# Differential attention with later transposes and one shared PSUM bank per head, and another order of the three branch projections

## The chip, the cores and the metric

The kernel runs on one core of one Trainium2 chip. The metric is the time of one execution on the device in microseconds (us). A core has five engines that run side by side, each through its own instructions in a fixed order: TensorE (PE, matmuls and transposes; its weight loads are the row PEld), VectorE (DVE), ScalarE (ACT), GpSimd (POOL) and SyncE (SP, here the queue that issues most loads). TensorE writes to PSUM, which has eight banks of 128 x 512 float32.

## The reference

One decoder layer on 512 tokens of width 1024. One projection `x @ w_in` gives the inputs of three token mixers and three gates. Their results are projected, gated and summed, and one more projection, a LayerNorm, an MLP with a gated embedding and a second LayerNorm follow. What the change touches is the first mixer, differential attention with 4 heads, and the sum of branches:

```python
prob = softmax(logits + bias)                       # two maps per head, causal
w = prob[:, :, 0] - lam * prob[:, :, 1]
o = einsum('bhqk,bhkd->bhqd', w, v)
o = o * rsqrt(mean(square(o), axis=-1) + RMS_EPS) * norm_g * (1.0 - lam_init)
...
merged = (g[:, :, 0] * (o_da @ w_branch_da) + g[:, :, 1] * (o_sb @ w_branch_sb)
          + g[:, :, 2] * (o_dl @ w_branch_dil))
```

The mean in the norm goes over the 128 columns of one token of one head.

## The kernel before, in words

The big products run as a list of **items**, in order: 128 x 512 results, each made by 24 matmuls for the input projection (three for each of 8 slices of the depth: high part times high part and the two cross terms, lines 86 to 89 and 299 to 301), or by 12 for a branch projection. Each item has `mm`, which issues its matmuls into one of two PSUM banks (tag `mm`), and `ev`, which evacuates the bank when the next item begins. Weights come through SP as 512 KB loads into a ring, and are split into a high and a low part by ACT (line 209) and DVE (line 210) some items ahead.

**Attention** is written as Python generators: `sb_head` (stick-breaking, 8), `dil_head` (dilated, 4) and `da_block` (differential attention, 4 heads of 4 query blocks of 128 tokens). A call of `step()` (line 1137) advances each active generator to its next `yield`, and admits one more from `waiting` if the estimates of PSUM banks in use (2 for a `da_block`) sum to no more than 8. `step()` is called once ahead of an item's matmuls and once in their middle (lines 1179 to 1183), so a `yield` puts about 12 matmuls between two parts of a block. All attention parts take their PSUM from a pool of six banks (tag `at`). A scheduling layer then fixes the order of each engine's instructions, and gives a PSUM bank or a slot of SBUF to each tile when its last user is done.

One `da_block(hd, qb)` does this. It makes the logits of both maps (lines 138 and 139, into two banks), adds the bias and takes row maxima (DVE, line 945), takes exponentials with row sums (ACT, line 951), and combines the maps (DVE, lines 954 to 957). After one `yield`, TensorE transposes the 128 x 128 blocks of the weights (line 961), ACT or DVE copies them to SBUF (`wT`, line 963, through lines 96 and 98). After another `yield`, TensorE multiplies by the values (line 969, `po`, a bank of its own for each block), ACT takes the sum of squares (`scr`, line 976), DVE, POOL and DVE turn it into the norm and scale the block (lines 977, 978, 979). When all four blocks of a head are done, TensorE transposes them (line 985), and ACT and DVE write the high and low part (lines 987, 988), which the branch projection reads.

`branch_items(j)` (line 347) appends three items for each of eight column tiles `j`: differential attention (i = 0), stick-breaking (1), dilated (2). Each `ev` takes a sigmoid of the gate (line 344, ordered behind the last exponential of line 951), multiplies (line 361) and adds (line 365); the third splits the sum (lines 370, 371). Six gate items (two column tiles) stand ahead of the first branch item, the other gate items follow between the branch items. At the first branch item (line 1158) all generators that are left are run to their end before the item is issued.

Of the kernel before, what the change touches and what calls it, by code (L numbers as in the profile page):

```python
# [12 lines left out]
AF = mybir.ActivationFunctionType  # L13
OP = mybir.AluOpType
# [3 lines left out]
P = 128  # L18
FF = 4096
ALPHA = 2.0 ** 0.25  # L20
EPS = 1e-5
# [34 lines left out]
def trunk(tc, a, out):  # L56
    nc = tc.nc
    es = ExitStack()
    with es:
# [23 lines left out]
        def at_bank():  # L83
            return psum.tile([P, 512], F32, name=nm("at"), tag="at", bufs=6)
# [80 lines left out]
        def chunk(src, w):  # L165
            return chunk_of(load(src, w))
# [58 lines left out]
        def item(cs, mm, ev, need=None, bank=None):  # L225
            items.append({"c": cs, "mm": mm, "ev": ev, "need": need, "bank": bank})
# [12 lines left out]
        V = {}  # L239
# [94 lines left out]
        oTs = {}  # L334
# [12 lines left out]
        def branch_items(j):  # L347
            c1 = chunk(a["wb1"][j].rearrange("p k m -> p (k m)"), 1024)
            c2 = chunk(a["wb2"][j].rearrange("p k m -> p (k m)"), 512)
            for i in range(3):  # L350
                def mm(ps, i=i):
                    c = c2 if i == 2 else c1
                    for k in range(4):
                        s = slice(((i % 2) * 4 + k) * P, ((i % 2) * 4 + k) * P + P)
                        h, lo = oTs[4 * i + k]
                        mm3(ps, c["h"][:, s], c["l"][:, s], h, lo, k == 0, k == 3)

                def ev(ps, i=i):
                    gate_sig(i, j)
                    g = sg.pop((i, j))  # L360
                    nc.vector.tensor_mul(g, g, ps)
                    if i == 0:
                        merged[j] = g
                    else:
                        nc.vector.tensor_add(merged[j], merged[j], g)
                    if i == 2:
                        m = merged[j]
                        h = slot("mh", F32R)
                        lo = slot("ml", F32R)
                        nc.scalar.copy(h, m)  # L370
                        nc.vector.tensor_sub(lo, m, h.bitcast(F32))
                        merged[j] = (h, lo)
                item([c1, c2] if i == 2 else [], mm, ev, need=[c1, c2])

        first_branch = [None]
        LEAD = 2
# [361 lines left out]
        ident = one.tile([P, P], F32, name="ident")  # L738
# [3 lines left out]
        mhalf = one.tile([P, 1], F32, name="mhalf")  # L742
# [79 lines left out]
        for i in range(2):  # L822
            nc.vector.scalar_tensor_tensor(lamt[:, 2 * i, :], lamt[:, 2 * i, :], 1.0, lamt[:, 2 * i + 1, :],
                                           op0=OP.mult, op1=OP.mult, accum_out=lp[:, i:i + 1])
# [103 lines left out]
            yield  # L928


        da_on = {}
        da_left = {}

        def da_block(hd, qb):
            while ("da_q", hd) not in T or ("da_k", hd) not in T:
                yield
            n = (qb + 1) * P
            nk = max(n, 256)
            lg, ssum, mx = [], small("ss", 2), small("mx", 2)
            for m in range(2):  # L940
                ps = at_bank()
                mm_pair(ps[:, :nk], T["da_q", hd], T["da_k", hd], m, slice(qb * P, qb * P + P), slice(0, nk),
                        True, True)
                t = slot("lg")[:, :n]
                nc.vector.tensor_tensor_reduce(out=t, in0=ps[:, :n], in1=tab_da[hd][:, 384 - 128 * qb:512],
                                               scale=1.0, scalar=-3.0e38, op0=OP.add, op1=OP.max,
                                               accum_out=mx[:, m:m + 1])
# [9 lines left out]
            nc.vector.scalar_tensor_tensor(lg[0], lg[0], r[:, 0:1], lg[1], op0=OP.mult, op1=OP.add)  # L957
            yield
            tp = at_bank()
            for b in range(qb + 1):  # L960
                nc.tensor.transpose(tp[:, b * P:b * P + P], lg[0][:, b * P:b * P + P], ident)
            wT = slot("wT")[:, :n]
            cp(wT, tp[:, :n])
            yield
            while ("da_v", 0, qb) not in V:
                yield
            po = at_bank()
            for kb in range(qb + 1):
                nc.tensor.matmul(po[:, :P], wT[:, kb * P:kb * P + P], V["da_v", 0, kb][:, hd * P:hd * P + P],
                                 start=kb == 0, stop=kb == qb)  # L970
            if hd not in da_on:
                da_on[hd] = slot("on")
                da_left[hd] = 4
            scr = one.tile([P, P], F32, name=nm("scr"), tag="scr", bufs=2)
            ss = small("ms", 1)
            nc.scalar.activation(scr, po[:, :P], AF.Square, accum_out=ss)
            nc.vector.tensor_scalar(ss, ss, 1.0 / P, EPS, op0=OP.mult, op1=OP.add)
            nc.gpsimd.tensor_tensor(ss, ss, mhalf, OP.pow)
            nc.vector.tensor_scalar(da_on[hd][:, qb * P:qb * P + P], po[:, :P], ss, None, op0=OP.mult)
            da_left[hd] -= 1  # L980
            yield
            if da_left[hd] == 0:
                tp = at_bank()
                for b in range(4):
                    nc.tensor.transpose(tp[:, b * P:b * P + P], da_on[hd][:, b * P:b * P + P], ident)
                h, lo = slot("oTh", F32R), slot("oTl", F32R)
                nc.scalar.activation(h, tp, AF.Copy, scale=gcol)
                nc.vector.scalar_tensor_tensor(lo, tp, gcol, h.bitcast(F32), op0=OP.mult, op1=OP.subtract)
                oTs[hd] = (h, lo)
                yield  # L990


        def dil_head(hd):
# [143 lines left out]
        def step():  # L1137
            clock[0] += 1
            if waiting and sum(e[0] for e in active) + waiting[0][0] <= BANKS and clock[0] - last[0] >= GAP[0]:
                active.append(waiting.popleft() + (clock[0],))  # L1140
                last[0] = clock[0]
            for e in list(active):
                if (clock[0] - e[3]) % e[2]:
                    continue
                try:
                    next(e[1])
                except StopIteration:
                    active.remove(e)
# [7 lines left out]
        prev = None  # L1156
        for n, it in enumerate(items):
            if n == first_branch[0]:
                while active or waiting:
                    step()  # L1160
            need = it["need"] or it["c"]
            while any("h" not in c for c in need):
                pump(freed, 1)
            if prev is not None:
                prev[0]["ev"](prev[1])
            pump(freed)
            if n == 14:
# [119 lines left out]
```

## Time and profile before

| what | value |
|---|---|
| three runs, median (lowest to highest) | 1104.25 us (1103.94 to 1104.48) |
| the profiled execution's own time | 1104.82 us |
| its span, first to last instruction | 1103.1 us |
| mean granted TensorE clock | 0.996 of full |
| PE busy | 1084.1 us (98%) |
| DVE, ACT, POOL busy | 682.4, 481.7, 38.8 us |
| first and last transpose of line 961 | 379.9 and 484.1 us |

A view of the profile groups instructions, or gives the busy time of each engine in a stretch of the span. Behind a bar or in brackets stands the idle time just before an instruction, and the engine, tile and line that ended it. A matmul of 512 columns is recorded with 0.39 us, but the next one starts about 0.23 us after it, since they are pipelined.

### The profile page before, as it was taken

The page shows a single profiled execution, that of the slowest core. Times are in us where ns is not written, and L with a number is a line of the kernel's source. Part 1 is how long each engine was busy: PE and PEld are TensorE (multiplying, and loading weights), DVE is VectorE, ACT ScalarE, POOL GpSimd, SP SyncE. Part 2 cuts the span into 40 slices and gives each one's busy share as a digit, 9 for nine tenths or more (in the row PEclk, how much of TensorE's full clock was granted, in tenths as well). Part 3 has the DMA queues.
Part 4 walks back from the last instruction along what each step waited for, and adds up shares of the span by engine and source line. Part 5 has one row for each costly group of instructions (what it writes and reads, how often), then busy time and mean ns, then how long its engine had stood idle before and what let it go on. Part 6 is the DMA issues. An engine that isn't in the chain of part 4 may idle for free.

```text
span 1103.1 us, 13166 instructions
## 1 busy us (share of the span) xinstructions
PE 1084.1 (98%) x5032; PEld 898.6 (81%) x5032; DVE 682.4 (62%) x1216; ACT 481.7 (44%) x803; POOL 38.8 (4%) x74
## 2 busy tenths in 40 slices
PE   8999999999999999899999999999999999999996
PEld 5888788999888887778888888888888888888884
DVE  6868466564253758654444354875676686686676
ACT  7656444343232545453233232333554454454433
POOL 1000200000000000000000020110000000000000
PEclk9999999999999999999999999999999999999999
DMA  8222422131222103113322344243222322322302
GB/s 271 103 96 84 135 77 77 39 102 50 98 77 87 59 27 105 58 52 102 105 86 96 105 143 163 77 153 113 97 96 77 134 96 80 131 96 95 115 1 76
DMA packets 31327, 105.71 MB, mean 96 GB/s; under 512 B 3962, under 2 KB 4106, under 8 KB 31264
## 3 DMA queue, kind: packets, MB, share of 16 engines
q1 hardware_dynamic: 28080, 96.48, 25.6%
q0 software_dynamic: 2608, 7.35, 2.2%
q10 hardware_dynamic: 576, 1.05, 0.3%
q8 instruction: 39, 0.64, 0.2%
q14 instruction: 24, 0.20, 0.1%
HBM read 102.74 MB, written 2.12 MB: 95 GB/s over the span
## 4 chain that ended last, share of the span: by engine, by line
PE 90%; DVE 5%; ACT 2%; issue 1%; DMA 1%; POOL 1%; SPq 0%; DVEq 0%; ACTq 0%; POOLq 0%
PE mm L88 17%; PE mm L89 17%; PE mm L87 17%; PE mm L299 3%; PE mm L301 3%; PE mm L300 3%; PE mm L632 2%; PE mm L631 2%; PE mm L633 2%; PE at L632 2%; PE at L631 2%; PE at L633 2%; PE mm L462 1%; PE mm L460 1%; PE mm L527 1%; PE mm L528 1%
## 5 line engine op out<-in xcount | busy, mean ns | idle before, releaser
L209 ACT CAST wh<-raw 128x1024 fp32r<-128x1024 f32 (+2 forms) x176 | 180.4, 1027 | 295.9 <-PE mm L88 237.9
L210 DVE TENSOR_TENSOR wl<-raw,wh 128x1024 fp32r<-128x1024 f32 (+2 forms) x176 | 209.0, 1192 | 120.8 <-ACT wh L209 119.2
L87 PE MATMUL mm<-xhT,wh 128*128 128x512 f32 x512 | 203.1, 397 | 0.9 <-DVE da_qb L108 0.7
L88 PE MATMUL mm<-xlT,wh 128*128 128x512 f32 x512 | 200.9, 392 | 1.6 <-DVE xlT L210 1.6
L89 PE MATMUL mm<-xhT,wl 128*128 128x512 f32 x512 | 201.2, 393 | 0.5 <-DVE wl L210 0.5
L88 PEld LDWEIGHTS mm<-xlT,wh 128*128 128x128 f32 x512 | 96.5, 188 | 22.4 <-DVE xlT L210 3.5
L87 PEld LDWEIGHTS mm<-xhT,wh 128*128 128x128 f32 x512 | 96.6, 189 | 20.6 <-DVE da_qb L108 1.1
L89 PEld LDWEIGHTS mm<-xhT,wl 128*128 128x128 f32 x512 | 96.3, 188 | 20.5 <-DVE wl L210 1.0
L88 PE MATMUL mm<-x1lT,wh 128*128 128x512 f32 x256 | 99.6, 389 | 0.0
L89 PE MATMUL mm<-x1hT,wl 128*128 128x512 f32 x256 | 99.6, 389 | 0.0
L87 PE MATMUL mm<-x1hT,wh 128*128 128x512 f32 x256 | 99.6, 389 | 0.0
L299 PE MATMUL mm<-wh,xhT 128*128 128x512 f32 x160 | 65.5, 410 | 0.0
L300 PE MATMUL mm<-wl,xhT 128*128 128x512 f32 x160 | 63.2, 395 | 0.0
L301 PE MATMUL mm<-wh,xlT 128*128 128x512 f32 x160 | 63.2, 395 | 0.0
L87 PEld LDWEIGHTS mm<-x1hT,wh 128*128 128x128 f32 x256 | 48.1, 188 | 10.0
L89 PEld LDWEIGHTS mm<-x1hT,wl 128*128 128x128 f32 x256 | 48.1, 188 | 10.0
L88 PEld LDWEIGHTS mm<-x1lT,wh 128*128 128x128 f32 x256 | 48.1, 188 | 9.9
L209 ACT CAST wh<-wsum 128x1024 fp32r<-128x1024 f32 x28 | 29.5, 1053 | 52.7 <-PE mm L88 49.3
L210 DVE TENSOR_TENSOR wl<-wsum,wh 128x1024 fp32r<-128x1024 f32 x28 | 34.3, 1224 | 23.7 <-ACT wh L209 23.1
L638 DVE TENSOR_TENSOR xn<-xn,mm 128x512 f32<-128x512 f32 x56 | 38.2, 682 | 9.9 <-PE mm L633 9.8
L632 PE MATMUL mm<-wl,hh 128*128 128x512 f32 x112 | 43.6, 389 | 0.0
L631 PE MATMUL mm<-wh,hh 128*128 128x512 f32 x112 | 43.6, 389 | 0.0
(302 smaller groups left out, 1948.9 us busy)
## 6 DMA issues: line engine op xcount, KB each, us to landing
raw<-in_wt_dram SPq DMA_DIRECT2D x63, 512.0 KB, 3.3
raw<-in_wu_dram SPq DMA_DIRECT2D x32, 512.0 KB, 3.3
raw<-in_wd_dram SPq DMA_DIRECT2D x32, 512.0 KB, 3.2
raw<-in_wv_dram SPq DMA_DIRECT2D x20, 512.0 KB, 3.3
raw<-in_wb_dram SPq DMA_DIRECT2D x8, 512.0 KB, 3.3
raw<-in_wo_dram SPq DMA_DIRECT2D x8, 512.0 KB, 3.6
raw<-in_wg_dram SPq DMA_DIRECT2D x8, 512.0 KB, 5.0
rawx<-in_xT_dram SPq DMA_DIRECT2D x8, 256.0 KB, 7.2
```

Of the source, the lines that this page charges most:

```text
L87: nc.tensor.matmul(ps, wh, xh, start=start, stop=False, skip_group_check=True)
L88: nc.tensor.matmul(ps, wh, xl, start=False, stop=False, skip_group_check=True)
L89: nc.tensor.matmul(ps, wl, xh, start=False, stop=stop, skip_group_check=True)
L209: nc.scalar.copy(h, raw)
L210: nc.vector.tensor_sub(lo, raw, h.bitcast(F32))
L299: nc.tensor.matmul(ps, x1, c["h"][:, s], start=k == 0, stop=False)
L300: nc.tensor.matmul(ps, x1, c["l"][:, s], start=False, stop=False)
L301: nc.tensor.matmul(ps, x2, c["h"][:, s], start=False, stop=k == 7)
L631: nc.tensor.matmul(ps, h[:, q], c["h"][:, s], start=go, stop=False, skip_group_check=True)
L632: nc.tensor.matmul(ps, h[:, q], c["l"][:, s], start=False, stop=False, skip_group_check=True)
L633: nc.tensor.matmul(ps, lo[:, q], c["h"][:, s], start=False, stop=end, skip_group_check=True)
L638: nc.vector.tensor_add(t, t, ps)
```

## The change

1. In `da_block`, the one `yield` between the combined weights and their transposes becomes three.
2. The four blocks of a head write their values into four quarters of one PSUM bank (`da_po[hd]`), which the head keeps until its norm is done. The sums of squares go into four columns of one tile. The scale is computed once per head: one DVE operation on 128 x 4, one POOL power on 128 x 4, and one DVE multiplication of 128 x 512 with the four columns broadcast. Two more `yield`s stand ahead of the head's transposes.
3. The branch items come in the order stick-breaking, dilated, differential attention.
4. At the first branch item only the results of the other two mixers are waited for; the generators left are run to their end at the third.

```diff
-            for i in range(3):
+            for n, i in enumerate((1, 2, 0)):
...
-                    if i == 0:
+                    if n == 0:
                         merged[j] = g
...
-                item([c1, c2] if i == 2 else [], mm, ev, need=[c1, c2])
+                item([c1, c2] if n == 2 else [], mm, ev, need=[c1, c2])
...
             nc.vector.scalar_tensor_tensor(lg[0], lg[0], r[:, 0:1], lg[1], op0=OP.mult, op1=OP.add)
-            yield
+            for _ in range(3):
+                yield
             tp = at_bank()
...
-            po = at_bank()
+            if hd not in da_po:
+                da_po[hd] = at_bank()
+                da_left[hd] = 4
+                da_ss[hd] = small("ms", 4)
+            po = da_po[hd]
+            qs = slice(qb * P, qb * P + P)
             for kb in range(qb + 1):
-                nc.tensor.matmul(po[:, :P], wT[:, kb * P:kb * P + P], V["da_v", 0, kb][:, hd * P:hd * P + P],
-                                 start=kb == 0, stop=kb == qb)
+                nc.tensor.matmul(po[:, qs], wT[:, kb * P:kb * P + P], V["da_v", 0, kb][:, hd * P:hd * P + P],
+                                 start=kb == 0, stop=kb == qb, skip_group_check=True)
...
-            nc.scalar.activation(scr, po[:, :P], AF.Square, accum_out=ss)
-            nc.vector.tensor_scalar(ss, ss, 1.0 / P, EPS, op0=OP.mult, op1=OP.add)
-            nc.gpsimd.tensor_tensor(ss, ss, mhalf, OP.pow)
-            nc.vector.tensor_scalar(da_on[hd][:, qb * P:qb * P + P], po[:, :P], ss, None, op0=OP.mult)
+            nc.scalar.activation(scr, po[:, qs], AF.Square, accum_out=ss[:, qb:qb + 1])
             da_left[hd] -= 1
-            yield
             if da_left[hd] == 0:
+                yield
+                nc.vector.tensor_scalar(ss, ss, 1.0 / P, EPS, op0=OP.mult, op1=OP.add)
+                nc.gpsimd.tensor_tensor(ss, ss, mhalf.to_broadcast([P, 4]), OP.pow)
+                on = slot("on")
+                nc.vector.tensor_mul(on.rearrange("p (b d) -> p b d", b=4), po.rearrange("p (b d) -> p b d", b=4),
+                                     ss.unsqueeze(2).to_broadcast([P, 4, P]))
+                yield
+                yield
                 tp = at_bank()
...
             if n == first_branch[0]:
+                while any(4 + k not in oTs for k in range(8)):
+                    step()
+            if n == first_branch[0] + 2:
                 while active or waiting:
                     step()
```

More of the change, by code (lines that the diff above doesn't have):

```diff
@@ L356, in mm, with ev @@
                         mm3(ps, c["h"][:, s], c["l"][:, s], h, lo, k == 0, k == 3)
-                def ev(ps, i=i):
+                def ev(ps, i=i, n=n):
                     gate_sig(i, j)
@@ L365, in ev @@
                         nc.vector.tensor_add(merged[j], merged[j], g)
-                    if i == 2:
+                    if n == 2:
                         m = merged[j]
@@ L928, in sb_head @@
             yield
-        da_on = {}
+        da_po = {}
+        da_ss = {}
         da_left = {}
@@ L966, in da_block @@
                 yield
-            po = at_bank()
-            for kb in range(qb + 1):
-                nc.tensor.matmul(po[:, :P], wT[:, kb * P:kb * P + P], V["da_v", 0, kb][:, hd * P:hd * P + P],
-                                 start=kb == 0, stop=kb == qb)
-            if hd not in da_on:
-                da_on[hd] = slot("on")
-                da_left[hd] = 4
-            scr = one.tile([P, P], F32, name=nm("scr"), tag="scr", bufs=2)
[L975 to L979, printed above, removed]
+            if hd not in da_po:
[4 more added lines that the diff above has]
+            qs = slice(qb * P, qb * P + P)
+            for kb in range(qb + 1):
+                nc.tensor.matmul(po[:, qs], wT[:, kb * P:kb * P + P], V["da_v", 0, kb][:, hd * P:hd * P + P],
+                                 start=kb == 0, stop=kb == qb, skip_group_check=True)
+            scr = one.tile([P, P], F32, name=nm("scr"), tag="scr", bufs=2)
+            ss = da_ss[hd]
+            nc.scalar.activation(scr, po[:, qs], AF.Square, accum_out=ss[:, qb:qb + 1])
             da_left[hd] -= 1
-            yield
             if da_left[hd] == 0:
+                yield
[6 more added lines that the diff above has]
+                yield
                 tp = at_bank()
                 for b in range(4):
-                    nc.tensor.transpose(tp[:, b * P:b * P + P], da_on[hd][:, b * P:b * P + P], ident)
+                    nc.tensor.transpose(tp[:, b * P:b * P + P], on[:, b * P:b * P + P], ident)
                 h, lo = slot("oTh", F32R), slot("oTl", F32R)
@@ L989, in da_block @@
                 oTs[hd] = (h, lo)
-                yield
+            yield
         def dil_head(hd):
```

## The prediction

> **What bounds the kernel now.** First the head of the page, then the busy times by stage.
>
> ```profile
> span 1103.1 us, 13166 instructions
> PE 1084.1 (98%) x5032; PEld 898.6 (81%) x5032; DVE 682.4 (62%) x1216; ACT 481.7 (44%) x803; POOL 38.8 (4%) x74
> ```
> ```profile
> core 0: us, PE busy (x) PEld busy (x) DVE busy (x) ACT busy (x) POOL busy (x), PEclk, DMA share, GB/s
> 0.00:379.00 379.00, 374.77 (x1835) 314.56 (x1836) 223.12 (x489) 177.68 (x316) 14.62 (x33) 1.00 0.29 98
> 379.00:490.00 111.00, 106.46 (x527) 85.55 (x527) 76.38 (x215) 57.66 (x145) 8.84 (x16) 0.98 0.18 62
> 490.00:700.00 210.00, 210.00 (x927) 173.61 (x926) 94.84 (x115) 66.89 (x86) 6.97 (x13) 1.00 0.35 115
> 700.00:1103.10 403.10, 392.89 (x1748) 324.86 (x1746) 288.01 (x400) 179.48 (x256) 8.40 (x12) 0.99 0.27 94
> ```
>
> TensorE is the bound. The change touches differential attention, which is the stretch 379 to 490. There TensorE idles 111.00 - 106.46 = 4.54 us, and the granted clock is 0.98. The branch stretch behind it has no idle time to win. So the question is how much of 379 to 490 is waiting, and whether the change removes it. The waits of TensorE name it (us in total, times, longest):
>
> ```profile
> PE at L961 <- DVE lg L957: 2.2, 5, 1.3
> PE at L969 <- DVE wT L98: 0.8, 1, 0.8
> PE mm L87 <- DVE da_qb L108: 0.7, 1, 0.7
> PE at L985 <- DVE on L979: 0.3, 1, 0.3
> ```
>
> The transposes wait for the combined weights, the value products for the copied transposes, one projection item for the evacuation of its bank, and a head's transposes for its norm. All four are heads of TensorE's queue: whatever stands behind them waits too, however ready it is.
>
> **Idle time is not all of a wait.** The next fences are the timeline of the last head and of the worst place.
>
> ```profile
> 485.23 1.16 PE L969 MATMUL at<-da_v,wT 128*128 128x128 f32 x8
> 486.65 0.26 ACT L976 ACTIVATE scr<-at 128x128 f32<-128x128 f32 x1
> 486.81 0.19 ACT L976 ACTIVATION_READ_ACCUMULATOR scr<-at 128x1 f32 x1
> 487.39 0.15 DVE L977 TENSOR_SCALAR ms<-ms 128x1 f32<-128x1 f32 x1
> 487.68 0.55 POOL L978 TENSOR_TENSOR ms<-ms,mhalf 128x1 f32<-128x1 f32 x1 [6.46 <-DVE ms L977]
> 487.95 0.39 PE L87 MATMUL mm<-xhT,wh 128*128 128x512 f32 x1
> 488.26 0.35 DVE L979 TENSOR_SCALAR on<-at,ms 128x128 f32<-128x128 f32 x1 [0.73 <-POOL ms L978]
> 488.67 0.33 PE L985 MATMUL at<-ident,on 128*128 128x128 f32 x1 [0.34 <-DVE on L979]
> 489.04 0.69 ACT L987 ACTIVATE oTh<-at,gcol 128x512 fp32r<-128x512 f32 x1 [2.04 <-PE at L985]
> 489.31 0.40 PE L87 MATMUL mm<-xhT,wh 128*128 128x512 f32 x1
> 489.54 0.40 PE L88 MATMUL mm<-xlT,wh 128*128 128x512 f32 x1
> 489.76 0.75 DVE L988 SCALAR_TENSOR_TENSOR oTl<-at,gcol,oTh 128x512 fp32r<-128x512 f32 x1 [1.15 <-ACT oTh L987]
> ```
>
> Two 512-column matmuls start 489.54 - 489.31 = 0.23 us apart, though each is recorded with 0.40. The transpose at 488.67 starts 0.72 after the matmul at 487.95, so 0.72 - 0.23 = 0.49 us are lost, of which the profile shows 0.34 as idle: 0.15 of each wait hides under the recorded tail of the matmul ahead of it.
>
> ```profile
> 450.10 0.40 PE L139 MATMUL at<-da_klb,da_qb 128*128 128x512 f32 x1
> 451.15 0.50 PE L87 MATMUL mm<-xhT,wh 128*128 128x512 f32 x1 [0.66 <-DVE da_qb L108]
> 452.98 0.35 DVE L979 TENSOR_SCALAR on<-at,ms 128x128 f32<-128x128 f32 x1 [0.16 <-POOL ms L978]
> 453.24 0.68 DVE L945 CUSTOM_DVE_ANT_0 lg<-at,shf 128x512 f32<-128x512 f32 x1
> 456.49 0.39 PE L89 MATMUL mm<-xhT,wl 128*128 128x512 f32 x1
> 457.25 0.75 DVE L957 SCALAR_TENSOR_TENSOR lg<-lg,rr,lg 128x512 f32<-128x512 f32 x1
> 458.15 0.63 PE L961 MATMUL at<-ident,lg 128*128 128x128 f32 x4 [1.28 <-DVE lg L957]
> 458.82 0.69 DVE L98 COPY wT<-at 128x512 f32<-128x512 f32 x1 [0.21 <-PE at L961]
> 459.56 0.38 PE L969 MATMUL at<-da_v,wT 128*128 128x128 f32 x1 [0.78 <-DVE wT L98]
> 460.30:463.70 3.40, 3.40 (x15) 3.11 (x15) 2.04 (x8) 0.48 (x2) 0.55 (x1) 0.50 0.27 102
> ```
>
> The last row is of the stage view; its 0.50 is the granted clock. From the last logits matmul at 450.10 the weights take until 457.25 + 0.75 = 458.00, 7.9 us, and TensorE had only 24 matmuls (5.5 us) to put between. It stood 1.28 us, then 0.78 us for the copy, and behind that the clock was at half for 3.40 us, which costs 3.40 x 0.50 = 1.7 us of work. [...] So the half clock belongs to these waits and goes with them.
>
> **The change, part by part.** All times are against the profiled execution (span 1103.1, its own time 1104.82); its time lies 0.57 above the median 1104.25, so I subtract the same gain from the median.
>
> *Three steps instead of one.* No instruction is added. The built order of both kernels shows what stands on TensorE between a four-block group's last logits matmul and its first transpose. At 0.23 us for a 512-column matmul, and less for shorter ones, it is for heads 0 to 3: before 6.4, 4.9, 5.5, 4.9 us, after 8.7, 9.5, 9.2, 8.2 us (head 3: 36 matmuls). The shorter blocks have 6.2 to 10.8 us after. What must fit in is the chain of lines 945 to 957: 7.9 us above at its worst, and at the last head
>
> ```profile
> 477.99 0.40 PE L139 MATMUL at<-da_klb,da_qb 128*128 128x512 f32 x1
> 482.99 0.75 DVE L957 SCALAR_TENSOR_TENSOR lg<-lg,rr,lg 128x512 f32<-128x512 f32 x1
> ```
>
> 482.99 + 0.75 - 477.99 = 5.8 us. So each cover is above the chain it must cover. The copies get cover too: at least 12 matmuls (2.7 us) stand between a transpose and its value product from head 1 on, against the 459.56 - 458.15 = 1.4 us that the worst one took. The price is that a block lives two steps longer and holds its slots; the built order shows no slot or bank of this stretch whose last user is a near neighbour of its next one on another engine, except the weight ring, as before.
>
> *One bank and one norm per head.* The rows (min/median/max ns) give the work:
>
> ```profile
> L977 DVE TENSOR_SCALAR ms<-ms x16: 144/154/156, 400.3 to 487.4; 128x1 f32<-128x1 f32 x16
> L978 POOL TENSOR_TENSOR ms<-ms,mhalf x16: 547/548/721, 400.5 to 487.7; 128x1 f32<-128x1 f32 x16
> L979 DVE TENSOR_SCALAR on<-at,ms x16: 347/351/353, 401.1 to 488.3; 128x128 f32<-128x128 f32 x16
> L361 DVE TENSOR_TENSOR graw<-graw,mm x24: 681/689/689, 501.1 to 661.6; 128x512 f32<-128x512 f32 x24
> ```
>
> DVE loses 16 x (0.15 + 0.35) = 8.1 us and gains 4 x (0.15 + 0.69) = 3.4 (line 361 is a 128 x 512 multiplication out of PSUM), so 4.7 less; POOL makes 4 powers instead of 16. Neither engine bounds this stretch (DVE 76 of 111), so this is worth nothing by itself. It clears DVE's queue ahead of line 945, where the last of three norms (452.98) stood just ahead of the logits of 450.10 (453.24). A power on 128 x 4 is not in the trace: 0.55 (the 128 x 1 row) to 4 x 0.55 = 2.2 if it went by elements; I take 0.65, near the row that differs only in three more elements per partition. It matters for the last head alone; elsewhere the order has 9 us between the last value product and the transposes.
>
> *Order of branches and the later flush.* The same items, matmuls, loads and evacuations. Twelve matmuls of stick-breaking and twelve of the dilated branch now stand between the last head's three steps. SP's loads keep their order; ACT still loads one sigmoid table, behind the last exponential, with five sigmoids ahead of the last square.
>
> **The sum.** Idle goes: 4.5. About 13 waits (five and three and some that show only at the weight loads) times 0.15 hidden: 2.0. Clock: 1.7. Together 8.2 us removable. What is late next is the last head. Its chain took 2.6 us before (last value product at about 486.12, transposes 488.67), and gets 0.34 for the wider multiplication and 0.1 for the power: 3.0 against the 12 matmuls, 2.7, so 0.3 lost. Its low part stands in DVE's queue behind a gate multiplication, an addition and a weight split (0.69 + 0.69 + 1.2), with 3.0 us of matmuls as cover: 0.2. Its last copy stands behind a weight split that waits for ACT's table load and sigmoids: 0.3 (0 to 1.3). Another 0.4 for waits that I cannot see. That leaves 1.2, and the gain is 8.2 - 1.2 = 7.0: 1104.25 - 7.0 = **1097.3 us**.
>
> **Rivals.**
>
> *The waits move to the last head.* If the power costs 2.2 us, or ACT reaches the last square late, two waits of 1.3 us come close together as at 458 to 460, and the clock halves again (1.7): 4.3 instead of 1.2 left, 1100.4 us. For it: that place has the thinnest cover of the new order. Against it: each of the three covers is within 0.3 us of its chain.
>
> *The shared bank gives it back.* With four blocks in one bank, a value product must wait until ACT has read the block ahead of it, although it writes other columns; the built order has that wait on ACT. Before, each block had its own bank. The square takes 0.26 + 0.19 us; behind a weight cast on ACT it would come about 1 us late. Twelve waits of 0.5 us return 6: 1103.3 us, no change. Against it: the closest two products of one head stand 2.0 us apart on TensorE. [...]
>
> *Slower: banks run short.* A head holds its bank for 20 us and more, and heads overlap. If a block's logits then find no free bank, TensorE's whole queue stands until line 945 has read one. Twelve blocks follow the first head; at 8.2 / 12 = 0.68 us each the gain is gone, and with 0.95 us each (the bank wait at 451.15 lost 1.05 - 0.23 = 0.8) 11.4 come back: 1107.5 us. Against it: in the built order a logits bank's former reader is well ahead.
>
> **How the numbers follow.** Forecast 0.70; last head 0.14; shared bank 0.06; slower 0.07; and 0.03 that more than 8.3 us go, by shorter switches between the two matmul kinds. The forecast's own range is 1095.9 (all 8.2 gone) to 1099.5 (3.4 left). To hold 8 in 10 it must take in the last head's case with the same spread: 1095.9 to 1101.5. A measurement tells 0.2% (2.2 us) from no change: faster 0.87, same 0.06, slower 0.07.
>
> **What would show it.** Right: between 379 and the end of differential attention no wait of line 962 and following for the combined weights, no half clock there, TensorE idle below 1.5 us in that stretch, the rest of the span the same within 1 us. Wrong: waits of the value products for ACT's square (shared bank), of the logits for line 946's bank (slower), or idle above 2 us around the first two branch items, with half clock (last head). A power of four columns above 1 us would show the last head's case from its cause.

## The result and the profile after

| | median | lowest to highest | runs |
|---|---|---|---|
| before | 1104.37 us | 1103.94 to 1106.86 | 4 |
| after | 1098.22 us | 1097.73 to 1099.55 | 4 |

The ratio is 0.9945 [0.9933, 0.9956]: 6.2 us faster, within the range, 0.9 us above the forecast. The profiled execution of after is the fastest of the four: 1097.73 us, its span 1095.7. The head of its page:

```profile
span 1095.7 us, 13124 instructions
PE 1079.6 (99%) x5032; PEld 898.3 (82%) x5032; DVE 676.9 (62%) x1192; ACT 482.2 (44%) x803; POOL 34.5 (3%) x62
```

Where the 7.4 us between the two profiled spans came from can be read off two instructions which both traces have: the first logits matmul of differential attention, and the last matmul of the branch projections (from the timelines of TensorE: start, duration, instruction). First before:

```profile
373.57 0.28 PE L138 MATMUL at<-da_ka,da_qa 128*128 128x256 f32 x1
661.16 0.39 PE L89 MATMUL mm<-oTh,wl 128*128 128x512 f32 x1
```

And after:

```profile
373.00 0.28 PE L138 MATMUL at<-da_ka,da_qa 128*128 128x256 f32 x1
653.95 0.39 PE L89 MATMUL mm<-oTh,wl 128*128 128x512 f32 x1
```

The stretch between them went from 287.59 to 280.95 us, 6.6 less. Ahead of it stands 0.6 less, behind it 0.2 less. Of the 6.6, the busy times by stage show how much was visible idling (columns as before: PE busy, PEld, DVE, ACT, POOL, granted clock, DMA):

```profile
379.00:490.00 111.00, 109.41 (x551) 91.06 (x550) 72.39 (x187) 60.23 (x147) 3.08 (x3) 1.00 0.20 67
```

TensorE's idle time fell from 4.54 to 111.00 - 109.41 = 1.59 us, 2.95 less; the half clock (1.7) is not there. The other 2.0 are what is left over by subtraction; the prediction's waits under the recorded tails of matmuls would fill them. What TensorE still waits for in this stretch:

```profile
PE at L976 <- ACT da_v L96: 0.8, 1, 0.8
PE at L976 <- DVE wT L98: 0.6, 1, 0.6
PE at L976 <- ACT wT L96: 0.2, 1, 0.2
```

Line 976 is the value product (969 before). The transposes (line 963, before 961) no longer wait for the combined weights, and the head's transposes (994) not for the norm. The last head, from the timeline:

```profile
493.87 1.01 POOL L986 TENSOR_TENSOR ms<-ms,mhalf 128x4 f32<-128x4 f32 x1 [21.46 <-DVE ms L985]
494.91 0.69 DVE L988 TENSOR_TENSOR on<-at,ms 128x512 f32<-128x512 f32 x1 [1.12 <-POOL ms L986]
495.75 0.62 PE L994 MATMUL at<-ident,on 128*128 128x128 f32 x4
```

The multiplication ends at 494.91 + 0.69 = 495.60, and TensorE arrives at 495.75: no wait, with 0.15 us to spare. VectorE, though, stood 1.12 us for POOL.

### The profile page after: what moved, and what is told of

The parts are those of the page before. It is cut to its first block, busy times and chain, and to the rows that moved or that the text cites. A ratio compares the mean times of both kernels' runs of the same rounds, so it can differ in the third digit from the quotient of the medians.

```text
span 1095.7 us, 13124 instructions
## 1 busy us (share of the span) xinstructions
PE 1079.6 (99%) x5032; PEld 898.3 (82%) x5032; DVE 676.9 (62%) x1192; ACT 482.2 (44%) x803; POOL 34.5 (3%) x62
## 4 chain that ended last, share of the span: by engine, by line
PE 92%; DVE 4%; ACT 2%; DMA 1%; issue 1%; SPq 1%; POOL 0%; DVEq 0%; ACTq 0%
PE mm L87 17%; PE mm L89 17%; PE mm L88 17%; PE mm L299 3%; PE mm L301 3%; PE mm L300 3%; PE mm L632 2%; PE mm L633 2%; PE mm L631 2%; PE at L632 2%; PE at L633 2%; PE at L631 2%; PE mm L462 1%; PE mm L460 1%; PE mm L528 1%; PE mm L526 1%
```

## The experiments

In the tables, "stretch" is the time between the two instructions shown above, in the profiled execution, and "half clock" the time at half clock within it. Each ratio is against the runs of before on the kernel's own chip. The first row is before as it was timed beside the kernels with e_steps in one block; before had a median of 1104.69 beside e_order and e_bank_order, and of 1104.37 beside after.

Executions of one kernel differ by some microseconds, and the long ones have the lower mean clock: of the 23 of before beside e_after_mult, the fastest took 1103.35 us at a granted clock of 0.998 and the slowest 1107.19 at 0.993. One stretch of 3.4 us at half clock costs 1.7 us of work, and some traces have one where others have none (last section), so I read the stretch beside the median. The stretch is that of one execution.

**The three parts, alone and in pairs.** S is the three steps (item 1 of the change), B the shared bank with one norm per head (item 2), O the order with the later flush (items 3 and 4).

| kernel | parts | median (lowest to highest) | ratio | stretch | half clock |
|---|---|---|---|---|---|
| before | - | 1104.8 (1103.19 to 1105.36) | 1 | 287.6 | 3.4 |
| e_steps | S | 1099.96 (1099.18 to 1101.48) | 0.9959 [0.9947, 0.9972] | 282.6 | 0 |
| e_bank | B | 1099.47 (1099.29 to 1101.13) | 0.9956 [0.9944, 0.9969] | 282.2 | 0 |
| e_order | O | 1104.71 (1103.37 to 1106.11) | 1.0001 [0.9993, 1.001] | 286.6 | 0 |
| e_steps_order | S, O | 1098.30 (1097.91 to 1099.89) | 0.9945 [0.9932, 0.9959] | 281.3 | 0 |
| e_bank_order | B, O | 1100.75 (1099.12 to 1100.95) | 0.9961 [0.9948, 0.9973] | 282.2 | 0 |
| e_steps_bank | S, B | 1102.53 (1100.93 to 1103.41) | 0.9980 [0.9972, 0.9989] | 284.2 | 0 |
| after | S, B, O | 1098.22 (1097.73 to 1099.55) | 0.9945 [0.9933, 0.9956] | 281.0 | 0 |

S or B alone brings about 5 us; S and B together, without O, bring 2.3 (e_steps_bank, below).

e_steps, three steps alone:

```diff
-            yield
+            for _ in range(3):
+                yield
             tp = at_bank()
```

> The kernel before with the three steps alone: own banks, four norms per head, old order of branches. Cover theory (the time goes where too few matmuls stand between a producer and TensorE's next use of it): the built order gives 6.2 to 10.8 us between logits and transposes, and 2.7 us or more to most value products, so those waits go; but the last head's transposes stand right behind its last value product (0.0 us), and a norm took 2.6 us there before. 2.6 us come back, perhaps with a half clock (1.7): 1101 us, at most 1103. One-norm theory (what helped is the work taken from DVE by the shared bank): most of the gain is missing, 1103 us or more, with DVE still late at the logits.

4.8 us faster: the cover theory's side, by a microsecond more.

e_bank, the second item of the change, with one step and the old order and flush:

```diff
-            po = at_bank()
+            if hd not in da_po:
+                da_po[hd] = at_bank()
...
-            nc.gpsimd.tensor_tensor(ss, ss, mhalf, OP.pow)
+                nc.gpsimd.tensor_tensor(ss, ss, mhalf.to_broadcast([P, 4]), OP.pow)
```

> The kernel before with the shared bank and one norm per head alone (with its two steps ahead of a head's transposes): one step from logits to transposes, old order of branches. Cover theory: the built order has 2.1 to 7.3 us between logits and transposes, as before; their waits stay (4 to 6 us lost in the stretch), the half clock probably too: 1103 to 1105 us. One-norm theory: DVE's queue is clear, the worst wait (1.28 us) goes, and half or more of the gain is there: 1099 to 1101 us.

5.3 us faster: the number of the one-norm theory, and not that of the cover theory, which was my prediction's. TensorE's waits are small (line 962 transposes the weights, 993 the head, 975 is the value product):

```profile
PE at L993 <- DVE on L987: 0.5, 1, 0.5
PE at L962 <- DVE lg L958: 0.3, 1, 0.3
PE at L975 <- DVE wT L98: 0.2, 1, 0.2
```

The trace shows two causes. At one block VectorE's queue got shorter, as the one-norm theory has it (timelines of TensorE and VectorE; line 945, here 946, reads the logits). First before:

```profile
409.59 0.28 PE L139 MATMUL at<-da_klb,da_qb 128*128 128x256 f32 x1
411.47 0.35 DVE L979 TENSOR_SCALAR on<-at,ms 128x128 f32<-128x128 f32 x1 [0.17 <-POOL ms L978]
411.73 0.41 DVE L945 CUSTOM_DVE_ANT_0 lg<-at,shf 128x256 f32<-128x256 f32 x1
415.19 0.44 PE L961 MATMUL at<-ident,lg 128*128 128x128 f32 x2 [0.32 <-DVE lg L957]
```

And e_bank:

```profile
409.27 0.28 PE L139 MATMUL at<-da_klb,da_qb 128*128 128x256 f32 x1
409.59 0.42 DVE L946 CUSTOM_DVE_ANT_0 lg<-at,shf 128x256 f32<-128x256 f32 x1 [0.17 <-PE at L139]
412.80 0.41 PE L962 MATMUL at<-ident,lg 128*128 128x128 f32 x2
```

In before, two norms stood ahead of the reading of the logits, and TensorE waited 0.32 us with 22 matmuls in between. Here none stands there, and the wait is gone with only 14 matmuls in between. But at the worst place of before (450.10 to 458.15) the chain got no shorter:

```profile
451.36 0.47 PE L139 MATMUL at<-da_klb,da_qb 128*128 128x512 f32 x1
458.60 0.74 DVE L958 SCALAR_TENSOR_TENSOR lg<-lg,rr,lg 128x512 f32<-128x512 f32 x1
459.40 0.66 PE L962 MATMUL at<-ident,lg 128*128 128x128 f32 x4 [0.27 <-DVE lg L958]
```

The weights take 458.60 + 0.74 - 451.36 = 8.0 us, as before (7.9), though no norm stands in VectorE's queue there: evacuations and casts do. What changed is the built order: 32 matmuls stand between where 24 stood, and the wait fell from 1.28 to 0.27 us. So e_bank is no test of the queue alone: its edit also moves the blocks against the matmuls (a head's last block lives two steps longer), and the largest wait went by more cover. How the 5.3 us divide between the two is not shown. What is shown is that steps and bank each take most of the same waits, and that they don't add up.

e_steps_order and e_steps_bank are the two pairs with S:

```diff
-            for i in range(3):
+            for n, i in enumerate((1, 2, 0)):
...
             if n == first_branch[0]:
+                while any(4 + k not in oTs for k in range(8)):
+                    step()
+            if n == first_branch[0] + 2:
```

> Three steps and the order of branches with the later flush, but each block with its own bank and its own norm. Cover theory: all covers are as in the changed kernel (2.5 to 3.4 us ahead of each head's transposes against a norm of 2.6 us), so it keeps nearly all of the gain: 1098 to 1099.5 us. One-norm theory: DVE has 4.7 us more work in the stretch and the norms stand ahead of the logits again: 1101 us or more.

As after, within what can be told apart: on top of steps and order the shared bank brings nothing.

> Three steps and the shared bank, with the old order of branches and the old flush. It differs from the changed kernel in the last head alone: 0.9 us instead of 2.7 from its last transposes to its value product, 1.1 instead of 2.7 to the head's transposes. Cover theory: the copy takes about 1.4 us and the norm 3.4 us (square 0.5, power 1.0, multiplication 0.7 and the ways between), so 0.5 and 2.3 us are lost there, 1101 us, and 1102.7 if the clock halves behind it. If the order of branches were only cosmetic: 1098.2 us.

1102.53, at the value named for the half clock. The profiled execution is a faster one, 1101.37 us, without half clock. Without the new order the last head has too few matmuls to hide its norm (its waits; 996 is the high part):

```profile
PE at L994 <- DVE on L988: 1.5, 1, 1.5
PE mm L87 <- ACT oTh L996: 0.8, 1, 0.8
```

e_order is the edit of e_steps_order without the steps.

> The kernel before with the new order of the branch items and the later flush alone (one step, a bank and a norm for each block). Cover theory: the order gives matmuls to the last head only, and the waits of the kernel before stand at the combined weights and their copies of earlier blocks (2.2 + 0.8 us idle, half clock behind them). These stay; the last head's wait (0.34 us idle, 0.49 lost) goes: 0.5 us less than before, between 0 and 1 less, within what can be told from no change. Rival: the order is worth by itself what it was worth on top of the other parts (1.7 us on three steps with own banks, 4.3 on three steps with the shared bank): 1.7 to 4.3 us less than before.

No difference, as the cover theory has it. The order is worth nothing where the waits stand at earlier blocks. By the medians it is worth 1.7 us on the steps, where the two intervals overlap, and 4.3 on steps and bank; by the stretches 1.3 and 3.2. The trace of e_order teaches something else. The worst place of before is there with the same two waits, yet the clock stays at full (timeline, then the stage):

```profile
458.49 0.63 PE L961 MATMUL at<-ident,lg 128*128 128x128 f32 x4 [1.24 <-DVE lg L957]
459.90 1.16 PE L969 MATMUL at<-da_v,wT 128*128 128x128 f32 x8 [0.78 <-DVE wT L98]
```
```profile
379.00:490.00 111.00, 106.38 (x534) 84.93 (x533) 77.48 (x219) 57.68 (x145) 8.85 (x16) 1.00 0.18 62
```

e_bank_order is after with one step:

```diff
-            for _ in range(3):
-                yield
+            yield
```

> The kernel after with one step instead of three between the weights and their transposes (shared bank, one norm per head, new order). The theory as it now stands: the three norms of a head ahead of line 946 in VectorE's queue made the chain long, and either remedy (more matmuls as cover, or a shorter queue) removes most of the same wait; so with the shared bank the three steps are worth nothing more, and the time is that of the kernel after within 1 us: 6 us less than before (5 to 7). Rival: the steps are what carries the kernel after, and the shared bank alone only happened to be well placed: without them 2 us or more are lost against after, 4 us less than before or fewer.

By its median the rival's number: 3.9 us faster than before. But where is the difference to e_bank? The stretch is that of e_bank, 282.2, and so are the three waits. What is longer lies at 114 us, ahead of every changed instruction: e_bank_order, then e_bank.

```profile
114.00:117.40 3.40, 3.40 (x10) 2.56 (x9) 0.00 (x0) 0.01 (x1) 2.67 (x5) 0.51 0.03 6
```
```profile
114.00:117.40 3.40, 3.40 (x18) 2.82 (x18) 0.00 (x0) 0.19 (x1) 2.69 (x6) 1.00 0.04 7
```

Without these 1.7 us the steps are worth 1.2 us on top of bank and order by the stretches (282.2 and 281.0), 1.4 by the fastest runs (1099.12 and 1097.73): neither 0 nor 2 or more.

**What the shared bank does without the one norm.** e_bank16 has four quarters of one bank, but 16 norms:

```diff
-            po = at_bank()
+            if hd not in da_po:
+                da_po[hd] = at_bank()
...
+            po = da_po[hd]
+            qs = slice(qb * P, qb * P + P)
-            nc.vector.tensor_scalar(da_on[hd][:, qb * P:qb * P + P], po[:, :P], ss, None, op0=OP.mult)
+            nc.vector.tensor_scalar(da_on[hd][:, qs], po[:, qs], ss, None, op0=OP.mult)
```

> The kernel before with the four blocks of a head in four quarters of one bank, but still a norm for each block (16 powers, 16 multiplications of 128 x 128), one step, old order. The shared bank with one norm per head was worth 5 us by itself; this run splits the two. Queue theory (the one norm shortens VectorE's queue ahead of the logits' reading; the bank itself is worth nothing): the norms still stand 6 us for POOL in VectorE's queue and the waits for the combined weights stay: within 1.5 us of before, the trace again with about 2 us of waits for the weights. Rival (the bank itself, since three banks of four come free earlier for logits and transposes): most of the 5 us, 1099 to 1101. A third case, the shared bank by itself costs time (a value product waits for the readers of its neighbours): 1 us or more slower than before.

1107.41 us (1106.96 to 1108.54), before 1104.27, ratio 1.003 [1.0018, 1.0041], stretch 289.6: the third case. TensorE's waits (975 is the value product, 982 the multiplication of the norm):

```profile
PE mm L87 <- DVE da_qb L108: 2.9, 1, 2.9
PE at L962 <- DVE lg L958: 2.4, 3, 1.5
PE at L975 <- DVE on L982: 0.7, 3, 0.3
```

The last line is new: a value product waits for the multiplication of a neighbour in its bank, which writes and reads other columns. These waits are only 0.7 us of the 7.27 that TensorE idles in the stretch (4.54 in before). The longest, 2.9 us for an evacuation, stands where the built order changed: in before three value products stood ahead of the projection item that waits, here one does, and the other two stand behind it. VectorE also comes to that evacuation 1.1 us later than in before. So the bank without the one norm costs 3 us, and one norm per head on it brings 8 (1107.41 to 1099.47; the two were timed on different chips, against 1104.27 and 1104.8). How the 3 us divide between the wait by bank and the order that follows from the edit is not shown.

**VectorE's wait for POOL.** e_pow3 adds three powers with exponent 1 to each head's norm in after:

```diff
                 nc.gpsimd.tensor_tensor(ss, ss, mhalf.to_broadcast([P, 4]), OP.pow)
+                for _ in range(3):
+                    nc.gpsimd.tensor_tensor(ss, ss, mone.to_broadcast([P, 4]), OP.pow)
```

> The kernel after with three more powers (exponent 1, 128 x 4 on POOL) in the norm of each head, one behind the other between the scale's power and the multiplication; nothing is left out, 12 operations are added. Each takes about 1.0 us on POOL by the row of the kernel after. The first three heads have 9 us of cover between the last value product and the transposes and should lose nothing; the last head had 0.15 us to spare, so TensorE should stand there about 3.0 - 0.15 = 2.9 us: 1101.1 where after is at 1098.2. If the clock falls to half when some 2 us of idle time lie within 3.4 us, as the trace of before suggests, 1.7 more: 1102.8. [...] Rival: the norm is not on the path (other work of the last head ends later): within 0.5 us of after.

1110.11 us (1107.65 to 1115.63), ratio 1.0055 [1.0037, 1.0074]: 12 us above after, not 3 to 5. The last head lost what was expected; two earlier ones, which I had held to be covered, lost nearly as much (TensorE's waits; 998 is the head's transposes, 978 the value product). The trace is of the slowest of the six executions, 1115.63 us, so its lines show where time goes, and not how much in the median:

```profile
PE at L998 <- DVE on L992: 3.1, 1, 3.1
PE at L978 <- DVE wT L98: 2.7, 1, 2.7
PE at L978 <- DVE rr L957: 1.8, 1, 1.8
```

VectorE's timeline at the earliest of the three, the one of 1.8 us, shows the cause:

```profile
426.08 0.69 DVE L992 TENSOR_TENSOR on<-at,ms 128x512 f32<-128x512 f32 x1 [4.32 <-POOL ms L990]
426.69 0.41 DVE L98 COPY wT<-at 128x256 f32<-128x256 f32 x1
427.02 0.16 DVE L957 RECIPROCAL rr<-ss 128x2 f32<-128x2 f32 x1
```

The multiplication stands 4.32 us at the head of VectorE's queue for POOL, and the copy that TensorE needs stands behind it. The copy began at 426.69, right behind the multiplication of 426.08, and the value product at 427.25, after TensorE's 1.83 us of waiting. My 9 us of cover were cover for the head's own transposes; I had not asked who else is in that queue.

e_pow3_mult keeps the three powers and moves only the multiplication, by one of the two steps behind it; TensorE's order is the same but for a handful of instructions. e_after_mult is the same edit on after:

```diff
                 on = slot("on")
+                yield
                 nc.vector.tensor_mul(on.rearrange("p (b d) -> p b d", b=4), po.rearrange("p (b d) -> p b d", b=4),
                                      ss.unsqueeze(2).to_broadcast([P, 4, P]))
                 yield
-                yield
```

> The run with three more powers lost not 3 us but 12 against the kernel after, and its trace shows why: VectorE's multiplication of the norm stands 4.3 us at the head of VectorE's queue for POOL, and reciprocals, scalings and copies of other blocks stand behind it, so that TensorE waits 2.0 and 2.8 us at two value products, with half clock behind each. Here the same three added powers stay, and only that multiplication is moved one step later (one of the two steps behind it now stands ahead of it): in the built order it moves behind some eight other VectorE instructions, and TensorE's order stays. Queue theory: the losses at the first three heads go; the last head still waits about 3.2 us, with or without a half clock of 1.7: 1101.5 to 1104 where after is at 1098.2 and the other run at 1110. Rival: the powers cost by their length on POOL's own path to the transposes: no change, 1108 to 1111.

1102.3 us (1100.16 to 1105.02), ratio 0.9979 [0.9971, 0.9988]: the queue theory's number, 7.8 us below e_pow3 for one moved instruction per head. The first three heads' multiplications no longer wait for POOL; the last head's does, 4.38 us, and TensorE's 3.1 stand there. The other 0.7 stand at the second head's transposes, for which the multiplication now comes late (TensorE's waits, VectorE's instruction at the first head, the stage of the last head):

```profile
PE at L998 <- DVE on L993: 3.8, 2, 3.1
```
```profile
426.27 0.69 DVE L993 TENSOR_TENSOR on<-at,ms 128x512 f32<-128x512 f32 x1
```
```profile
490.00:510.00 20.00, 16.91 (x82) 13.87 (x81) 9.86 (x14) 6.64 (x11) 4.03 (x4) 1.00 0.21 66
```

> The kernel after with only this edit: the norm's multiplication one step later, behind some eight other VectorE instructions. VectorE then no longer stands 1.1 us for POOL at each of four heads (4.3 us in all). Queue theory: in the kernel after no wait of TensorE over 0.2 us is left behind these stands (what is left stands behind exponentials on ScalarE and evacuations on VectorE), so the gain is small: 0 to 0.5 us less than after, 1097.7 to 1098.4; the last head ends as before. Rival: the order of copies shifts (one value product has only 0.9 us of matmuls behind its transposes in the built order, where it had 3.0): up to 1 us more than after.

1097.65 us (1097.19 to 1099.15), ratio 0.9934 [0.9921, 0.9947], stretch 280.7: at the lower end of the queue theory's expectation, and the fastest version of the study, but its interval overlaps that of after. That it beats after is not shown. Its trace shows a trade: the wait of 0.6 us for a copy is gone, and one of 0.7 stands at the second head's transposes, which wait for the multiplication.

e_mult_step tries the same on before:

```diff
             nc.gpsimd.tensor_tensor(ss, ss, mhalf, OP.pow)
+            yield
             nc.vector.tensor_scalar(da_on[hd][:, qb * P:qb * P + P], po[:, :P], ss, None, op0=OP.mult)
```

> The kernel before with one edit: in each block, one step between POOL's power and VectorE's multiplication. Nothing of the rest of the change: one step ahead of the transposes, a bank and a norm for each block, old order. By the trace of before VectorE stands 6.2 us for POOL at 13 of 16 norms, and three norms in a row hold its queue from 451.13 to 453.24 while the logits of 450.10 wait for it; the waits of 1.28 and 0.78 us and the half clock stand behind that. Queue theory: with the multiplications out of the way these waits go and most of what the shared bank with one norm was worth (5 us) comes from this edit alone: 3 to 5 us less than before. Rival (number of operations): the 16 multiplications still stand in the queue, only elsewhere, and what one norm saved was their number: within 1.5 us of before.

1102.9 us (1101.73 to 1104.14), ratio 0.998 [0.9971, 0.9988]: 1.9 us, between the two. It is no clean test: VectorE's waits for POOL, which the edit was to remove, hardly fell. Before, then here:

```profile
DVE on L979 <- POOL ms L978: 6.2, 13, 0.7
```
```profile
DVE on L980 <- POOL ms L978: 5.8, 11, 0.7
```

The stretch is 285.4 us, 2.2 less than in before, and 1.7 of these are the half clock that this trace does not have. So what the 16 waits cost in before, apart from the number of the norms, stays open.

**A try at the rest.** e_vla_b13 gives the value products of after one step more, and lets six blocks be active instead of four:

```diff
                 yield
+            yield
             if hd not in da_po:
...
-                waiting.append((2, da_block(hd, qb), DA_PERIOD))
+                waiting.append((1.33, da_block(hd, qb), DA_PERIOD))
```

> The kernel after with one more step between the transposes of the weights (with their copy) and the value product, for all blocks, and an estimate of 1.33 banks instead of 2 for a differential block, so that six instead of four are active at once and the longer blocks do not end later. What the kernel after still loses in this stretch (about 2.1 us) stands by the trace at the value products, which wait for the copies of lines 96 and 98 behind other work of ScalarE and VectorE; with 12 more matmuls of cover (at least 19 us of matmuls where there were 2.1) these waits should go: 1.9 us less than after, 1096.3 where after is at 1098.2. Rival: with six blocks active the banks of the pool run short or the vector engines bunch, and the logits wait for a bank: no gain or up to 3 us more than after.

1101.9 us (1100.84 to 1102.61), ratio 0.9973 [0.9962, 0.9983], stretch 283.6: the rival's side, 3.7 us above after. The waits at the value products went, but one came at the transposes, with a half clock behind it:

```profile
PE at L963 <- DVE lg L958: 1.8, 1, 1.8
```
```profile
446.90:450.30 3.40, 1.49 (x9) 0.92 (x8) 3.24 (x6) 3.35 (x7) 0.00 (x0) 1.00 0.00 0
450.30:453.70 3.40, 3.40 (x10) 2.65 (x9) 3.37 (x6) 1.34 (x3) 0.00 (x0) 0.50 0.00 1
```

VectorE and ScalarE were busy 3.24 and 3.35 of the 3.40 us ahead of it: the blocks bunch. Which of the two edits does that was not tried.

## Why the prediction was right, and where it was not

- **The bound and what could be won: right.** The waits of the transposes for the combined weights went and the half clock with them; outside the stretch 0.8 us changed. Of the 6.6 won in the stretch, 2.95 were idle time (4.5 in the sum), 1.7 the clock, and 2.0 are left, the size that the sum gave to waits hidden under matmul tails. The idle time left, 1.59 us, is just above the 1.5 that I had named as the sign of being right. (The lower end of the range is off by its own sum: 1104.25 - 8.2 is 1096.05 and not 1095.9.)
- **Three steps as cover: right** (e_steps, e_steps_order), but with some luck at the first head. I took the chain to be 7.9 us at its worst; in after it takes 9.3 there (387.83 to 397.10). TensorE's own work up to the transposes at 397.89 is 9.2 us, without the 0.82 us that it stood for a value's evacuation in between; without that other wait it would have come at about the same time as the weights.
- **"Worth nothing by itself", of the shared bank with one norm: wrong.** This is the step that failed. Alone it is worth 5.3 us (e_bank). I priced VectorE's busy time against its share of the stretch, 76 of 111 us, and noted beside it that the norms stand just ahead of the logits' reading, but gave that no price. The block at 409 us shows what that left out: with the norms out of the queue the first transpose comes 3.5 us behind the last logits matmul instead of 5.6, and TensorE's wait is gone. I also took TensorE's order to stay; at the worst place it got 32 matmuls of cover for 24. An engine that is two thirds busy on average can be the late one at the place where TensorE waits. The sum came out because steps and bank remove the same wait, so that one of them was enough; the forecast did not depend on the term that was wrong.
- **The rival of the shared bank: right that a wait by bank exists, wrong in its place.** It comes through the multiplications and not through ACT's square as I wrote: 0.7 us at three value products in e_bank16. That run costs 3 us as a whole, and how much of it is this wait is open. The one norm per head takes these readers away: no value product of after waits for a multiplication.
- **The copies' cover: wrong.** "At least 12 matmuls between a transpose and its value product" did not do. Two of the waits that are left, 0.6 and 0.2 us, are value products that wait for their copies, which stand behind evacuations and casts on VectorE and behind exponentials on ACT. The largest, 0.8 us at the first head, has no term in the sum: the values themselves are late, since their evacuation (`da_v`) stands behind two exponentials on ACT. Of the 1.2 us that the sum left over, 0.8 were put at the last head, which lost nothing, and 0.4 at waits not seen. What is left is 1.6 us idle and, with 0.15 hidden at each of three waits, 2.1; the difference of 0.9 is the size of what the forecast fell short by.
- **The power of four columns: mis-sized.** 0.65 taken, 1.01 measured. The sign that I named for the last head's case was there, and the case did not come: 0.15 us were to spare. e_pow3_mult shows that it was close: 3 us more on POOL are 3.1 us of wait.
- **The order: right**, that it serves the last head only (e_order: nothing; e_steps_bank: 4.3 us above after without it).
- **The half clock "goes with these waits": too firm.** All that before shows is that it stood behind them, from 460.3 us on for 3.40. In the two traces compared it goes, but e_order has the same waits (1.24 and 0.78 us) without it. How much of the difference between the medians it is, no run shows.
- **The slower rival** left no trace: after shows no wait of logits for a bank.

## What to carry to other kernels

A wait at the head of TensorE's queue was here the producer's chain minus the matmuls in between (at the worst place of before 7.9 us and 5.5; of the 2.4 between them 0.8 were lost at another wait and 1.28 stood idle), so it can be mended at either end, and two mends of one wait did not add (4.8 and 5.3 us alone, 2.3 together): try each alone. Then count in the trace both the chain and the matmuls in between, since an edit at one end can move the other (e_bank). Price an edit on a helper engine by what stands behind it in that engine's queue at the place where the bound engine waits, not by busy shares; where an instruction stands for microseconds for a third engine, try to issue it a step later. Before you explain a microsecond of difference between two medians, look whether it lies where the kernels differ.

## What was not expected of the hardware

**The half clock went by windows of 3.41 us.** In the trace of e_pow3 it begins at 12.12, 114.52, 428.55, 459.27 and 510.47 us. The last four lie 30, 122, 131 and 146 times 3.4133 us behind the first, so these beginnings lie on one grid. So do the two in the trace of before, at 460.29 us and, behind the last matmul, at 1098.58: 187 times 3.4133 us lie between them. In e_pow3 the half clock lasted one such window from 428.55 on, and two from 459.27 and from 510.47 on (stage view, cut by the grid):

```profile
507.05:510.46 3.41, 1.22 (x6) 0.68 (x4) 0.00 (x0) 1.04 (x1) 3.17 (x4) 1.00 0.00 0
510.47:517.29 6.82, 5.94 (x16) 4.89 (x17) 3.77 (x5) 0.69 (x1) 0.01 (x1) 0.50 0.15 41
```

The five windows ahead of a half clock in differential attention (before, e_vla_b13, three in e_pow3) held 1.8 to 2.2 us of idle time. The grid may also be why like waits stand ahead of a half clock in before and not in e_order. The waits of 1.28 and 0.78 us of before fall into one window, which holds 3.41 - 1.35 = 2.06 us of idle time; in e_order their like fall across its edge, and the window holds 3.41 - 1.87 = 1.54. Before, then e_order with the window behind, which is at full clock:

```profile
456.87:460.28 3.41, 1.35 (x11) 1.14 (x11) 3.13 (x6) 2.64 (x5) 0.00 (x0) 1.00 0.20 50
```
```profile
457.73:461.14 3.41, 1.87 (x15) 1.66 (x15) 3.17 (x5) 2.20 (x5) 0.00 (x0) 1.00 0.36 106
461.14:464.55 3.41, 3.29 (x18) 2.36 (x17) 2.19 (x11) 1.30 (x4) 0.55 (x1) 1.00 0.14 53
```

But in these traces idle time alone does not decide. The 3.09 us of e_pow3_mult's last head fall into two windows, of which the second holds 3.41 - 1.50 = 1.91 us, as much as the one in e_vla_b13, and the clock stays at full (the first of the next two fences). And e_bank_order's window ahead of 114.09 us has no idle time at all and is followed by half clock. It holds all ten matmuls of line 769, whose weights are 33 x 4 where the projection's are 128 x 128. So it is, to 0.04 us, in all four traces with half clock there (e_steps, e_bank_order, e_pow3, e_after_mult); in the other ten the grid cuts through these matmuls (in before at 112.13 us, where they run from 110.91 to 113.66; in after at 111.48, where they run from 110.34 to 113.09). The two fences are e_pow3_mult and e_bank_order:

```profile
497.16:500.57 3.41, 1.50 (x9) 1.36 (x10) 2.31 (x4) 0.69 (x1) 1.01 (x1) 1.00 0.00 0
500.57:503.98 3.41, 3.41 (x17) 2.81 (x16) 2.26 (x4) 1.05 (x1) 0.00 (x0) 1.00 0.24 77
```
```profile
110.68:114.09 3.41, 3.41 (x14) 1.24 (x13) 0.00 (x0) 1.89 (x5) 1.26 (x3) 1.00 0.44 156
```

What exactly counts in a window, no run here shows.

**A power on 128 x 4 took 1.01 us on POOL**, on 128 x 1 0.55: neither the same price nor four times as much; by these two rows I estimate (1.01 - 0.55) / 3, some 0.15 us, for each further column.
